# Two rows of the last chunk but one, stored by thirteen masked indirect transfers

## The chip, the cores and the metric

The kernel runs on one core of one Trainium2 chip. The metric is device time in microseconds of one execution; each comparison is between medians of several executions. The core has the engines that the profile calls DVE (VectorE), ACT (ScalarE), POOL (GpSimd), SP (SyncE, used here only to issue transfers) and PE (TensorE, unused here), and sixteen DMA engines that carry all transfers between the chip's main memory and the on-chip buffer of 128 partitions.

## What is computed

A softmax over rows of logits of shape (2, 8, 2112, 2112), after a bias that depends on the head and on the distance of row and column, clipped at 16:

```python
pos = np.arange(S)
rel_clipped = np.clip(pos[:, None] - pos[None, :], -16, 16) + 16
logits = logits + rel_bias[:, rel_clipped][None]
logits = logits - logits.max(axis=-1, keepdims=True)
exp = np.exp(logits)
return exp / exp.sum(axis=-1, keepdims=True)
```

All in float32. Every logit is read once and every result written once: 285 MB each way.

## The kernel before

The 33,792 rows are dealt out so that each partition owns 264 consecutive rows (`ROWS`). A chunk is six rows of each partition (`R`), 6,336 KB, and there are 44 chunks (`N`), numbered 0 to 43. Four buffers `X[0]` to `X[3]` (`NBUF`) hold chunks in turn; results are written in place, so a buffer is loaded, worked on, and stored from.

Work on a chunk: DVE adds the bias strip `F` and takes the negated row maximum (`add`, line 181), ACT exponentiates with the row sum as by-product (`exps`, line 190), DVE takes reciprocals and multiplies, three rows to a group (`scale`, lines 198 and 202). Each scaled row adds one to the semaphore `scaled`. Ahead of the loop DVE builds the bias table `M` from `rel_bias`, which ACT's queue loads at line 108; POOL contributes two index tables (lines 112 and 113).

All large transfers are issued by SP, in an order written out by hand. It loads chunk 0 row by row (line 99) and chunks 1 to 3 (line 103). Then it stores chunk 0: five rows of every partition in one transfer, and the sixth row by seventeen smaller ones, listed in `FAN`, of 15, 14, 13 ... 1 partitions, one row each (lines 223 to 232). Then a loop (line 233): store the next chunk when it is scaled, wait until the chunk stored before has landed (`st`), load the chunk that takes its buffer. After the loop stand the stores of chunks 41 and 42 (lines 238 and 239) and of chunk 43 in two halves of three rows (lines 240 and 241), so that the first half goes while the second is being scaled. `store` (line 91) waits on `scaled` and then issues. At the end SP waits for the stores still under way, last for the two halves on `landed` (line 244).

POOL, after its two index tables, waits for chunk 0's stores (lines 114 to 116) and passes that on to SP as `st[0]` (line 117). It has nothing after that.

Of the kernel before, what the change touches and what calls it, by code (L numbers as in the profile page):

```python
# [8 lines left out]
I32 = mybir.dt.int32  # L9
EXP = mybir.ActivationFunctionType.Exp  # L10
ALU = mybir.AluOpType
# [4 lines left out]
def kernel(  # L16
# [6 lines left out]
    nc = tc.nc  # L23
    P = 128
    B, H, S, S2 = logits.shape
# [3 lines left out]
    ROWS = B * H * S // P  # L29
    PB = S // ROWS  # L30
    assert ROWS * P == B * H * S and PB * ROWS == S and PB == H == 8
    R = 6
    NBUF = 4
    STEP = R * NBUF
    N = ROWS // R
# [2 lines left out]
    MW = S + ROWS - 1  # L38
    FW = S + STEP - 1
    BIG = 3.0e38  # L40
    LANES = 9
    FAN = []
    for lane in range(LANES):
        m = len(range(lane, P, LANES))
        k = 15 if lane == 0 else 15 - lane
# [4 lines left out]
    io = ctx.enter_context(tc.tile_pool(name="io", bufs=1))  # L50
    X = [io.tile([P, R * S], FP32, tag=f"X{b}", name=f"X{b}") for b in range(NBUF)]
# [2 lines left out]
    nmax = io.tile([P, STEP], FP32, tag="nmax", name="nmax")  # L54
    tot = io.tile([P, STEP], FP32, tag="tot", name="tot")
    rec = io.tile([P, STEP], FP32, tag="rec", name="rec")
    ip = io.tile([P, 3, PB], I32, tag="ip", name="ip")
    ps = ctx.enter_context(tc.tile_pool(name="ps", bufs=1, space=bass.MemoryType.PSUM))
    M = ps.tile([P, 4096], FP32, tag="M", name="M")

    def view(t, offset, dims):

        return bass.AP(tensor=t.tensor, offset=t.offset + offset, ap=[[list(t.ap[0])[0], P]] + dims)

    def rows(t, j, n):

        return bass.AP(tensor=t.tensor, offset=t.offset + j * S, ap=[[ROWS * S, P], [1, n * S]])

    with tc.tile_critical(no_gpsimd_drain=True):
        ld = [nc.alloc_semaphore(f"ld{b}") for b in range(NBUF)]  # L70
        st = [nc.alloc_semaphore(f"st{b}") for b in range(NBUF)]
        added = nc.alloc_semaphore("added")
        expd = nc.alloc_semaphore("expd")
        scaled = nc.alloc_semaphore("scaled")
# [2 lines left out]
        pre = nc.alloc_semaphore("pre")  # L77
        idx = nc.alloc_semaphore("idx")
        dve = nc.alloc_semaphore("dve")
        main = nc.alloc_semaphore("main")  # L80
        fan = [nc.alloc_semaphore(f"fan{i}") for i in range(2)]
        landed = tc.alloc_semaphore("landed")

        def take(eng, sem, n):
            eng.wait_ge(sem, n).then_inc(sem, -n)  # L85


        def load(j, b):
            nc.sync.dma_start(out=X[b][:, :], in_=rows(logits, j, R)).then_inc(ld[b], 16)

        def store(j, b, s0=0, n=R, sem=None):
            take(nc.sync, scaled, n)
            nc.sync.dma_start(
                out=rows(out, j + s0, n), in_=X[b][:, s0 * S : (s0 + n) * S]
            ).then_inc(sem or st[b], 16)


        for r in range(R):
            nc.sync.dma_start(
                out=X[0][:, r * S : (r + 1) * S], in_=rows(logits, r, 1)  # L100
            ).then_inc(ld[0] if r == R - 1 else pre, 16)
        for n in range(1, NBUF):
# [6 lines left out]
            out=rbB,  # L109
            in_=bass.AP(tensor=rel_bias.tensor, offset=rel_bias.offset, ap=[[0, P], [1, H * W]]),  # L110
        ).then_inc(rb, 16)
        nc.gpsimd.iota(ip[:, 0], pattern=[[0, PB]], base=0, channel_multiplier=1).then_inc(idx, 1)
        nc.gpsimd.iota(ip[:, 2], pattern=[[1, PB]], base=0, channel_multiplier=0).then_inc(idx, 1)  # L113
        take(nc.gpsimd, main, 16)
        take(nc.gpsimd, fan[0], 16 * ((len(FAN) + 1) // 2))
        take(nc.gpsimd, fan[1], 16 * (len(FAN) // 2))
        nc.gpsimd.sem_inc(st[0], 16)

        v = nc.vector
        done = [0]  # L120

        def then(ins):
            done[0] += 1
            ins.then_inc(dve, 1)

        def settle():
            v.wait_ge(dve, done[0])
# [6 lines left out]
                             op0=ALU.logical_shift_right, op1=ALU.bitwise_and))  # L134
# [6 lines left out]
        settle()  # L141
        for m, op in ((eq, ALU.is_equal), (gt, ALU.is_gt), (le, ALU.is_le), (lt, ALU.is_lt)):
            then(v.tensor_scalar(out=m, in0=dp, scalar1=0.0, scalar2=None, op0=op))  # L143
        v.wait_ge(rb, 16)
        settle()
        then(v.tensor_tensor(  # L146
            out=view(F, 0, [[W, H], [1, W]]), in0=view(F, 0, [[W, H], [1, W]]),
            in1=view(F, SC + 3 * PB, [[1, H], [0, W]]), op=ALU.mult))
        settle()
        then(v.tensor_reduce(out=rbS[:, :], in_=view(F, 0, [[1, W], [W, H]]),  # L150
                             axis=mybir.AxisListType.X, op=ALU.add))
# [5 lines left out]
            out=view(F, 0, [[W, PB], [1, W]]), in0=view(F, SC + 2 * PB, [[1, PB], [0, W]]),  # L157
            in1=view(rbS, W - 1, [[0, PB], [-1, W]]), op=ALU.mult))
# [6 lines left out]
            out=view(M, U, [[ROWS, PB], [1, W]]), in0=view(F, 0, [[W, PB], [1, W]]),  # L165
            in1=view(F, SC + 8 * PB, [[1, PB], [0, W]]), op=ALU.add))
        then(v.tensor_copy(out=view(M, U + W, [[ROWS, PB], [1, ROWS - W]]),  # L167
                           in_=view(F, SC + 7 * PB, [[1, PB], [0, ROWS - W]])))
# [8 lines left out]
        def add(b):  # L177
            take(v, ld[b], 16)
            for r in range(b * R, (b + 1) * R):
                x = X[b][:, (r - b * R) * S : (r - b * R + 1) * S]  # L180
                v.tensor_tensor_reduce(  # L181
                    out=x, in0=x, in1=F[:, STEP - 1 - r : STEP - 1 - r + S], scale=-1.0, scalar=BIG,
                    op0=ALU.add, op1=ALU.min, accum_out=nmax[:, r : r + 1],
# [37 lines left out]
        for i, (k, g, lane) in enumerate(FAN):  # L221
            p = g * LANES + lane
            nc.sync.dma_start(
                out=bass.AP(
                    tensor=out.tensor, offset=out.offset + (p * ROWS + R - 1) * S,
                    ap=[[LANES * ROWS * S, k], [1, S]],
                ),
                in_=bass.AP(
                    tensor=X[0].tensor, offset=X[0].offset + p * PSX + (R - 1) * S,
                    ap=[[LANES * PSX, k], [1, S]],  # L230
                ),
            ).then_inc(fan[i % 2], 16)
        with nc.Fori(0, ROWS - 2 * STEP + 1, STEP, engines=[ENG.SP]) as j:
            for b in range(NBUF):
                store(j + (b + 1) * R, (b + 1) % NBUF)
                take(nc.sync, st[b], 16)
                load(j + (b + NBUF) * R, b)
        for n in range(N - NBUF + 1, N - 1):
            store(n * R, n % NBUF)
        store((N - 1) * R, (N - 1) % NBUF, 0, HALF, landed)  # L240
        store((N - 1) * R, (N - 1) % NBUF, HALF, R - HALF, landed)
        for b in range(NBUF - 1):
            take(nc.sync, st[(N + b) % NBUF], 16)
    nc.sync.wait_ge(landed, nc.sync.to_reg(32), synchronizes=[nc.sync.lower_ap(out)])


# [28 lines left out]
```

## Time and profile before

| | us |
|---|---|
| median of 3 runs | 1331.55 |
| lowest and highest | 1331.31, 1331.82 |
| the profiled execution's own time | 1331.3 |
| its span, first to last instruction | 1329.5 |
| DVE busy | 976.7 |
| ACT busy | 575.2 |
| POOL busy | 0.4 |

The rows of the profile are shown in the prediction. How they read: the page begins with the span, then gives for each engine the busy time, its share and the number of instructions; a line of forty digits or numbers cuts the span into forty equal slices (a digit 9 is 90% busy or more; GB/s is what the DMA engines moved). A DMA queue's line has packets, MB and the share of sixteen engines' time; q1 is SP's queue and q10 ACT's. A packet is here one partition's part of a transfer, or the 4 bytes by which a DMA engine counts up a semaphore when its part is done. In a window's row stand the stretch (us from the span's start), its length, the busy time of DVE, ACT and POOL with their instructions, the clock of PE, the mean share of the sixteen DMA engines, and GB/s. In the timeline SPq and ACTq are the sequencers that issue transfers. A row of issues has the size of one transfer and the median time from issue to landing.

### The profile page before, as it was taken

How to read it: one execution, taken by the hardware profiler on the slowest of the kernel's cores; microseconds unless marked ns; L12 is line 12 of the kernel's file. 1: busy time of each engine (PE TensorE's matmuls, PEld its weight loads, DVE VectorE, ACT ScalarE, POOL GpSimd, SP SyncE). 2: the span in 40 equal slices, each digit the busy share in tenths (PEclk: the TensorE clock that was granted, in tenths of full speed). 3: DMA queues.
4: the chain of work that ended last, by engine and by line, in shares of the span. 5: the costliest groups of instructions: out<-in, count | busy, mean ns of one | idle time of the engine just before them, and what ended most of it. 6: DMA issues, size and time to landing. Idle time of an engine off the chain costs nothing. (4 is left out here: it accounts for less than half of the span.)

```text
span 1329.5 us, 2477 instructions
## 1 busy us (share of the span) xinstructions
DVE 976.7 (73%) x911; ACT 575.2 (43%) x539; POOL 0.4 (0%) x6
## 2 busy tenths in 40 slices
DVE  5998767777877776787778767677877776687772
ACT  2565333444444343345444333444444343345440
POOL 0000000000000000000000000000000000000000
DMA  9999999999999999999999999999999999999997
GB/s 391 427 426 424 436 430 433 438 433 435 432 435 435 433 436 430 436 433 435 430 433 439 433 433 427 439 435 432 433 432 438 430 433 430 436 430 436 438 432 337
DMA packets 13939, 571.12 MB, mean 430 GB/s; under 512 B 1648, under 2 KB 1776, under 8 KB 1776
## 3 DMA queue, kind: packets, MB, share of 16 engines
q1 hardware_dynamic: 13792, 570.96, 99.5%
q10 hardware_dynamic: 144, 0.14, 0.1%
q14 instruction: 3, 0.02, 0.0%
HBM read 285.61 MB, written 285.47 MB: 430 GB/s over the span
## 5 line engine op out<-in xcount | busy, mean ns | idle before, releaser
L181 DVE CUSTOM_DVE_ANT_0 X<-X,F 128x2112 f32<-128x2112 f32 x264 | 605.2, 2354 | 302.0 <-DVEq L85 302.0
L190 ACT ACTIVATE X<-X,nmax 128x2112 f32<-128x2112 f32 x264 | 541.7, 2052 | 538.2 <-ACTq L85 516.4
L202 DVE TENSOR_SCALAR X<-X,rec 128x2112 f32<-128x2112 f32 x264 | 332.5, 1316 | 13.2
L190 ACT ACT_TABLE_LOAD x11 | 14.1, 1283 | 185.8 <-ACTq L85 185.8
L190 ACT ACTIVATION_READ_ACCUMULATOR X<-X,nmax 128x1 f32 x264 | 49.2, 186 | 0.0
L175 DVE COPY F<-M 128x2135 f32 x11 | 26.1, 2375 | 6.6 <-DVEq L85 6.6
L181 DVE DVE_READ_ACCUMULATOR2_ANT nmax<- 128x1 f32 x264 | 21.7, 82 | 0.0
L198 DVE RECIPROCAL rec<-tot 128x3 f32<-128x3 f32 x88 | 15.0, 170 | 0.0
L146 DVE TENSOR_TENSOR F<-F 128x264 f32<-128x264 f32 x1 | 0.4, 435 | 4.9 <-DMA F<-in_rel_bias_dram 4.9
L167 DVE COPY M<-F 128x1848 f32<-128x1848 f32 x1 | 2.1, 2077 | 0.0
L133 DVE TENSOR_SCALAR ip<-ip 128x8 int32<-128x8 int32 x1 | 0.2, 172 | 1.3 <-POOL ip L113 1.3
L150 DVE TENSOR_REDUCE rbS<-F 128x33 f32<-128x264 f32 x1 | 0.6, 610 | 0.0
L164 DVE TENSOR_TENSOR M<-F 128x264 f32<-128x264 f32 x1 | 0.4, 441 | 0.0
L156 DVE TENSOR_TENSOR F<-F,rbS 128x264 f32<-128x264 f32 x1 | 0.4, 426 | 0.0
L143 DVE TENSOR_SCALAR F<-F 128x8 f32<-128x8 f32 x4 | 0.4, 167 | 0.0
L169 DVE COPY M<-rbS 128x247 f32<-128x247 f32 x1 | 0.4, 406 | 0.0
L154 DVE TENSOR_SCALAR F<-F,rbS 128x8 f32<-128x8 f32 x1 | 0.2, 231 | 0.0
L160 DVE SCALAR_TENSOR_TENSOR F<-F,rbS 128x8 f32<-128x8 f32 x1 | 0.2, 227 | 0.0
L155 DVE TENSOR_SCALAR F<-F,rbS 128x8 f32<-128x8 f32 x1 | 0.2, 225 | 0.0
L161 DVE SCALAR_TENSOR_TENSOR F<-F,rbS 128x8 f32<-128x8 f32 x1 | 0.2, 221 | 0.0
L136 DVE TENSOR_TENSOR F<-ip 128x8 f32<-128x8 int32 x1 | 0.2, 167 | 0.0
L139 DVE TENSOR_TENSOR F<-ip 128x8 f32<-128x8 int32 x1 | 0.2, 167 | 0.0
(9 smaller groups left out, 1.2 us busy)
## 6 DMA issues: line engine op xcount, KB each, us to landing
X<-in_logits_dram SPq DMA_DIRECT2D x43, 6336.0 KB, 44.7
out_dram<-X SPq DMA_DIRECT2D x42, 6336.0 KB, 52.8
X<-in_logits_dram SPq DMA_DIRECT2D x6, 1056.0 KB, 12.6
out_dram<-X SPq DMA_DIRECT2D x2, 3168.0 KB, 21.9
out_dram<-X SPq DMA_DIRECT2D x1, 5280.0 KB, 34.9
F<-in_rel_bias_dram ACTq DMA_DIRECT2D x1, 132.0 KB, 6.4
out_dram<-X SPq DMA_DIRECT2D x1, 123.8 KB
out_dram<-X SPq DMA_DIRECT2D x1, 115.5 KB
```

What stands on the lines that cost most here:

```text
L143: then(v.tensor_scalar(out=m, in0=dp, scalar1=0.0, scalar2=None, op0=op))
L146: then(v.tensor_tensor(out=view(F, 0, [[W, H], [1, W]]), in0=view(F, 0, [[W, H], [1, W]]), in1=view(F, SC + 3 * PB, [[1, H], [0, W]]), op= ...
L150: then(v.tensor_reduce(out=rbS[:, :], in_=view(F, 0, [[1, W], [W, H]]), axis=mybir.AxisListType.X, op=ALU.add))
L156: then(v.tensor_tensor(out=view(F, 0, [[W, PB], [1, W]]), in0=view(F, SC + 2 * PB, [[1, PB], [0, W]]), in1=view(rbS, W - 1, [[0, PB], [-1, ...
L164: then(v.tensor_tensor(out=view(M, U, [[ROWS, PB], [1, W]]), in0=view(F, 0, [[W, PB], [1, W]]), in1=view(F, SC + 8 * PB, [[1, PB], [0, W]] ...
L167: then(v.tensor_copy(out=view(M, U + W, [[ROWS, PB], [1, ROWS - W]]), in_=view(F, SC + 7 * PB, [[1, PB], [0, ROWS - W]])))
L169: then(v.tensor_copy(out=M[:, 0:U], in_=low.to_broadcast([P, U])))
L175: v.tensor_copy(out=F[:, :], in_=M[:, bass.ds(ROWS - STEP - j, FW)]).then_inc(dve, 1)
L181: v.tensor_tensor_reduce(out=x, in0=x, in1=F[:, STEP - 1 - r : STEP - 1 - r + S], scale=-1.0, scalar=BIG, op0=ALU.add, op1=ALU.min, accum_ ...
L190: nc.scalar.activation(out=x, in_=x, func=EXP, scale=-1.0, bias=nmax[:, r : r + 1], accum_out=tot[:, r : r + 1],).then_inc(expd, 1)
L198: v.reciprocal(out=rec[:, r0 : r0 + HALF], in_=tot[:, r0 : r0 + HALF]).then_inc(inv, 1)
L202: v.tensor_scalar_mul(out=x, in0=x, scalar1=rec[:, r : r + 1]).then_inc(scaled, 1)
```

## The change

Of chunk 42, the last but one, SP stores only the first four rows of each partition. The last two rows (`PAIR`) go by POOL's queue in thirteen indirect transfers. Each takes 16 consecutive partitions, from `p0` on, and writes for each of them one piece of two rows (16.5 KB) to the row pair of the output that an index table names. Element e of a transfer is partition p0 + e. A mask of 16 bits for each transfer says which of its elements are wanted; the index of the others is raised by `FAR`, over the bound, and an index over the bound is passed over without an error. The thirteen ranges overlap, and each of the 128 partitions is wanted exactly once, so the list `PLAN` settles at which place e of a transfer each partition's piece goes.

The tables are made at the start: POOL writes masks and indices by 13 memsets and 14 iotas, DVE waits for them and then shifts, masks, multiplies and subtracts in four small instructions, ahead of its wait for the bias. POOL waits on a new semaphore, `ready`, which SP raises when chunk 42 is scaled, and issues the thirteen transfers. SP waits at the end for their 13 x 16 counts on `soft` too.

```diff
+    PLAN = [(0, 49095), (3, 26631), (12, 65472), (23, 55264), (34, 65509), (45, 32736), (54, 65472),
+            (65, 64480), (75, 15873), (81, 65287), (92, 57312), (103, 31716), (112, 65474)]
+    PAIR = 2
+    FAR = 1 << 20
+    assert sorted(p0 + e for p0, m in PLAN for e in range(16) if m >> e & 1) == list(range(P))
...
+        g = nc.gpsimd
+        BLK = ROWS // PAIR
+        AT = ((N - 1) * R - PAIR) // PAIR
+        made = [0]
+
+        def step(ins):
+            made[0] += 1
+            ins.then_inc(pool, 1)
+
+        for w, (p0, m) in enumerate(PLAN):
+            step(g.memset(bit[:, w : w + 1], m))
+            step(g.iota(sel[:, w : w + 1], pattern=[[0, 1]], base=p0 * BLK + AT + FAR, channel_multiplier=BLK))
+        step(g.iota(lan[:, :], pattern=[[0, len(PLAN)]], base=0, channel_multiplier=1))
         take(nc.gpsimd, main, 16)
         take(nc.gpsimd, fan[0], 16 * ((len(FAN) + 1) // 2))
         take(nc.gpsimd, fan[1], 16 * (len(FAN) // 2))
         nc.gpsimd.sem_inc(st[0], 16)
+        take(g, ready, 1)
+        pairs = out.rearrange("b h s t -> (b h s t)").rearrange("(n c) -> n c", c=PAIR * S)
+        late = X[(N - 2) % NBUF]
+        lap = list(late.ap[0])[0]
+        for w, (p0, m) in enumerate(PLAN):
+            g.indirect_dma_start(
+                out=pairs, out_offset=bass.IndirectOffsetOnAxis(ap=sel[:, w : w + 1], axis=0),
+                in_=bass.AP(tensor=late.tensor, offset=late.offset + p0 * lap + (R - PAIR) * S,
+                            ap=[[lap, 16], [1, PAIR * S]]),
+                in_offset=None, bounds_check=B * H * S // PAIR - 1, oob_is_err=False,
+            ).then_inc(soft, 16)
...
+        take(v, pool, made[0])
+        then(v.tensor_tensor(out=bit[:, :], in0=bit[:, :], in1=lan[:, :], op=ALU.logical_shift_right))
+        settle()
+        then(v.tensor_scalar(out=bit[:, :], in0=bit[:, :], scalar1=1, scalar2=None, op0=ALU.bitwise_and))
+        settle()
+        then(v.tensor_scalar(out=bit[:, :], in0=bit[:, :], scalar1=FAR, scalar2=None, op0=ALU.mult))
+        settle()
+        then(v.tensor_tensor(out=sel[:, :], in0=sel[:, :], in1=bit[:, :], op=ALU.subtract))
         v.wait_ge(rb, 16)
...
-        for n in range(N - NBUF + 1, N - 1):
+        for n in range(N - NBUF + 1, N - 2):
             store(n * R, n % NBUF)
+        take(nc.sync, scaled, R)
+        nc.sync.sem_inc(ready, 1)
+        nc.sync.dma_start(
+            out=rows(out, (N - 2) * R, R - PAIR), in_=X[(N - 2) % NBUF][:, 0 : (R - PAIR) * S]
+        ).then_inc(st[(N - 2) % NBUF], 16)
         store((N - 1) * R, (N - 1) % NBUF, 0, HALF, landed)
         store((N - 1) * R, (N - 1) % NBUF, HALF, R - HALF, landed)
         for b in range(NBUF - 1):
             take(nc.sync, st[(N + b) % NBUF], 16)
+    nc.sync.wait_ge(soft, nc.sync.to_reg(16 * len(PLAN)), synchronizes=[nc.sync.lower_ap(out)])
     nc.sync.wait_ge(landed, nc.sync.to_reg(32), synchronizes=[nc.sync.lower_ap(out)])
```

More of the change, by code (lines that the diff above doesn't have):

```diff
@@ L56 @@
     rec = io.tile([P, STEP], FP32, tag="rec", name="rec")
+    sel = io.tile([16, len(PLAN)], I32, tag="sel", name="sel")
+    bit = io.tile([16, len(PLAN)], I32, tag="bit", name="bit")
+    lan = io.tile([16, len(PLAN)], I32, tag="lan", name="lan")
     ip = io.tile([P, 3, PB], I32, tag="ip", name="ip")
@@ L79 @@
         dve = nc.alloc_semaphore("dve")
+        ready = nc.alloc_semaphore("ready")
+        pool = nc.alloc_semaphore("pool")
+        soft = tc.alloc_semaphore("soft")
         main = nc.alloc_semaphore("main")
```

## The prediction

> **What bounds the kernel now.** I read the page first, then SP's waits, then the end of the timeline, and last the final ten microseconds in slices. The page (span, busy times, DMA by fortieths of the span, queues), then SP's longest waits:
>
> ```profile
> span 1329.5 us, 2477 instructions
> DVE 976.7 (73%) x911; ACT 575.2 (43%) x539; POOL 0.4 (0%) x6
> DMA  9999999999999999999999999999999999999997
> GB/s 391 427 426 424 436 430 433 438 433 435 432 435 435 433 436 430 436 433 435 430 433 439 433 433 427 439 435 432 433 432 438 430 433 430 436 430 436 438 432 337
> q1 hardware_dynamic: 13792, 570.96, 99.5%
> ...
> SPq L244 <- DMA out_dram<-X: 14.6, 1, 14.6
> ```
>
> No compute engine is full; the sixteen DMA engines are, 99.5% of the span on SP's queue alone, at some 430 GB/s. Only the last fortieth is lower (337 GB/s), and the program ends by a wait of SP for the last store. So the time is the bytes at that rate plus what is lost at the two ends; bytes do not change here, so the change can act only at the ends. The end on the timeline:
>
> ```profile
> 1238.15 0.35 SPq L89 DMA_DIRECT2D X<-in_logits_dram  x1
> 1244.93 60.38 SPq L93 DMA_DIRECT2D out_dram<-X  x4
> ...
> 1271.08 3.78 DVE L202 TENSOR_SCALAR X<-X,rec 128x2112 f32<-128x2112 f32 x3
> 1283.08 2.36 DVE L181 CUSTOM_DVE_ANT_0 X<-X,F 128x2112 f32<-128x2112 f32 x1 [8.22 <-DVEq L85]
> ...
> 1297.08 3.78 DVE L202 TENSOR_SCALAR X<-X,rec 128x2112 f32<-128x2112 f32 x3
> ...
> 1301.09 3.78 DVE L202 TENSOR_SCALAR X<-X,rec 128x2112 f32<-128x2112 f32 x3
> ```
>
> The last load, issued at 1238.15, has landed at 1283.08; the last chunk but one is scaled at 1271.08 + 3.78 = 1274.9 and the last chunk at 1304.9, when SP issues its last half. From there only transfers run. Their end in slices (the last two columns are the DMA engines' mean share and GB/s), then the packets that start after 1320, then those of one late microsecond:
>
> ```profile
> 1316.00:1318.00 2.00, 0.00 (x0) 0.00 (x0) 0.00 (x0) 1.00 0.97 418
> 1318.00:1320.00 2.00, 0.00 (x0) 0.00 (x0) 0.00 (x0) 1.00 1.09 469
> 1320.00:1321.00 1.00, 0.00 (x0) 0.00 (x0) 0.00 (x0) 1.00 0.77 329
> 1321.00:1322.00 1.00, 0.00 (x0) 0.00 (x0) 0.00 (x0) 1.00 0.59 253
> 1322.00:1323.00 1.00, 0.00 (x0) 0.00 (x0) 0.00 (x0) 1.00 0.41 177
> 1323.00:1324.00 1.00, 0.00 (x0) 0.00 (x0) 0.00 (x0) 1.00 0.41 177
> 1324.00:1325.00 1.00, 0.00 (x0) 0.00 (x0) 0.00 (x0) 1.00 0.24 101
> 1325.00:1326.00 1.00, 0.00 (x0) 0.00 (x0) 0.00 (x0) 1.00 0.18 76
> 1326.00:1327.00 1.00, 0.00 (x0) 0.00 (x0) 0.00 (x0) 1.00 0.06 25
> 1327.00:1328.00 1.00, 0.00 (x0) 0.00 (x0) 0.00 (x0) 1.00 0.06 25
> 1328.00:1329.50 1.50, 0.00 (x0) 0.00 (x0) 0.00 (x0) 1.00 0.00 0
> ...
> DMA packets 63, 1.17 MB, mean 123 GB/s; under 512 B 17, under 2 KB 17, under 8 KB 17
> q1 hardware_dynamic: 63, 1.17, 28.5%
> ...
> DMA packets 1, 0.03 MB, mean 25 GB/s; under 512 B 0, under 2 KB 0, under 8 KB 0
> q1 hardware_dynamic: 1, 0.03, 5.9%
> ```
>
> This is the point on which all else hangs. A share is booked to the slice in which a packet starts, which is why one reads 1.09. Up to 1320 all sixteen engines work; then they run out one after another, and from 1326 on a single one works (0.06 is one sixteenth). One packet of a half store, 24.75 KB (three rows), takes 5.9% of 16 engines in 1 us: 0.94 us. The last starts after 1327, so the last engine ends at about 1328.1, and 1.4 us follow to the span's end. The same work spread evenly: packets starting after 1320 are 28.5% of 16 engines over 9.5 us, so 0.285 x 9.5 = 2.71 us for each engine, plus on average half a packet (0.47) under way at 1320: 1323.2. **4.9 us of the end is imbalance between DMA engines.**
>
> **The change part by part.** *Removed from SP's queue:* two of six rows of the last store but one, on every engine alike. *Added:* the same rows on POOL's queue, 128 pieces of two rows (16.5 KB), handed out by the table's masks. Counted by bit, engines 0 to 15 get 5, 4, 5, 0, 0, 6, 10, 10, 11, 12, 10, 12, 12, 11, 11, 9 pieces, where each had 8. A piece is two thirds of the packet above: 0.63 us. An engine that gets none ends 8 x 0.63 = 5.0 us sooner: the latest, 1328.1, comes to 1323.1. An engine that gets twelve ends 4 x 0.63 = 2.5 us later: those that run dry first, about 1320.9, come to 1323.4. So the table's extremes agree with the windows' extremes, and its sum is that of an even end near 1323.2.
>
> Does it hit the right engines? No view names an engine. The packet records behind the views can be followed, since on one engine each starts as its predecessor ends, and engines told apart by how many of the one-row pieces of the FAN stores each moved. The latest ends then lie on the engines that get fewest pieces, the earliest on those that get most; the exception is an engine that ends late and still gets ten. This moves my chances only.
>
> *Misfit.* That engine ends where the share drops from 0.41 to 0.24, at about 1324.1; two pieces more make it 1325.4. Lags of other executions will differ a little too, and now many engines stand near the maximum instead of one. Bounds: 0 (even end) to 2.0 (that engine alone sets the end, against 1323.4). I take 0.9, since not each execution need have such an engine.
>
> *Packets.* Each piece and each of thirteen completions costs something fixed. The only second queue with small packets is ACT's, in the first 20 us:
>
> ```profile
> q10 hardware_dynamic: 144, 0.14, 4.5%
> ```
>
> 4.5% of 16 engines over 20 us is 14.4 us for 144 packets, 0.10 each, 0.04 of it bytes at the rate above. So at most 0.06 x 25 = 1.5 us on an engine with twelve pieces, at least nothing; I take 0.3, being nearer to the low end because these packets are sixteen times as large and their neighbours sit in a full queue.
>
> *Issue by POOL.* No row shows a transfer issued by POOL. Nearest rows: SP's issue, and the store and half stores from issue to landing:
>
> ```profile
> L93 SPq DMA_DIRECT2D out_dram<-X x5: 332/337/338, 1215.0 to 1305.0; - x5
> ...
> out_dram<-X SPq DMA_DIRECT2D x1, 6336.0 KB, 38.6
> out_dram<-X SPq DMA_DIRECT2D x2, 3168.0 KB, 21.9
> F<-in_rel_bias_dram ACTq DMA_DIRECT2D x1, 132.0 KB, 6.4
> ```
>
> Low: 0.34 us each, 4.4 us in all. High: POOL handles one only after the other has landed, 6.4 us as for ACT's small load, 83 us. POOL is released at 1274.9 and the last piece must be through by 1323.2; with one SP packet ahead (0.94) and its own 0.63 that leaves 1321.6 - 1274.9 = 46.7 us, 3.6 us each. Below that the issue costs nothing, hidden by SP's backlog; from 4.0 us each ((1328.1 - 1.6 - 1274.9) / 13) the change loses. I take 1.5 us each, nearer to SP's row, since nothing in the code makes POOL wait for a landing: the last is issued at 1294.4. Without the cover of the backlog it would cost 19.5 us plus.
>
> [...]
>
> *Moved past the last load.* The pieces enter from 1274.9, while the last load (landed 1283.08) is on the engines, and may delay it by at most their whole work, 5.0 us a mean engine; then the first half store goes at about 1305.9 instead of 1300.9. The store issued at 1274.95 lands 38.6 us later, at 1313.5; with a third of its 15 us gone, 1308.5. The queue stays covered by 2.6 us. Cost: nothing; without that cover up to 5.0.
>
> *Added waits.* POOL's wait for "ready" holds only the thirteen transfers. SP's wait is that of the removed store. The wait at the end for "soft" stands beside the one for the last halves.
>
> *Start.* 27 small POOL instructions and four DVE instructions ahead of the bias:
>
> ```profile
> 1.04 0.13 POOL L112 IOTA ip<- 128x8 int32 x1 [0.59 <-PEq L270]
> 1.13 0.14 POOL L113 IOTA ip<- 128x8 int32 x1
> ...
> 2.07 0.39 DVE L143 TENSOR_SCALAR F<-F 128x8 f32<-128x8 f32 x4
> 7.39 0.43 DVE L146 TENSOR_TENSOR F<-F 128x264 f32<-128x264 f32 x1 [4.93 <-DMA F<-in_rel_bias_dram]
> ...
> 19.04 2.38 DVE L175 COPY F<-M 128x2135 f32 x1 [6.58 <-DVEq L85]
> ```
>
> 27 x 0.14 = 3.8 us after 1.3 gives 5.1; four dependent steps of about 0.2 give 5.9, before the bias lands at 7.39. Were it later, DVE still has 6.58 us idle ahead of 19.04. Cost: nothing, up to 8 us of delay.
>
> *Sum.* Last transfer: 1323.4 + 0.9 + 0.3 = 1324.6 against 1328.1: 3.5 us less. The profiled execution took 1331.3 us (span 1329.5 and 1.8 around it), so 1327.8; the median of the runs is 1331.55, 0.25 above it, so **1328.1**.
>
> **Rivals.** *The table does not steer (slower).* If the slots that the masks refuse are dropped before the transfer is shared out, the first engines get a piece of nearly every transfer; if they are moved all the same, every engine gets thirteen. Either way the latest engine has 13 pieces for 8: 5 x 0.63 = 3.15 us more, **1334.7**. It decides as soon as the latest engine gets more than eight. For it: no refused slot is in the trace. Against: the masks fit the slices' ends, which a compacted share would make pointless.
>
> *POOL is too slow (slower).* At 5 us an issue the last one comes at 1274.9 + 65 = 1339.9 and ends 1.6 us later, 13.4 us after 1328.1: **1345**. For it: nothing of POOL's DMA is seen. Against: it needs more than 4.0 us, twelve times SP's 0.34.
>
> *POOL is shut out while DVE works.* Add and scale fill DVE from 1283.08 to 1304.87. If POOL issues nothing in that time, four go before (8.2 us at 2 us, a high choice) and nine after, to 1322.9, ending at 1324.5: still hidden, a gain of 3.5. [...]
>
> *The lags are not the same each time (no change).* If they reshuffle, some engine with ten to twelve pieces is 3 to 4 us late and ends near 1327.5: **1330.9**. For it: the one exception. Against: three runs within 0.5 us, as if one engine set the end each time.
>
> **How the numbers follow.** Forecast 0.62, table not steering 0.13, POOL too slow 0.12, lags reshuffled 0.13; the shut-out belongs to the forecast. About 0.2% (2.7 us, below 1328.9) can be told from no change. Nine tenths of the forecast and a little of the rest are faster: 0.57; slower are the two slow rivals with a little of the reshuffle: 0.26; 0.17 remains. The forecast's own range is 1326.6 (the even end, a gain of 4.9) to 1330.3 (misfit 2.0 and packets 1.5: an end at 1326.9). The whole range reaches up to the table that doesn't steer: 1326.6 to 1334.8.
>
> **What would show it.** Right: the slices after 1320 hold full share to about 1322.5 and fall to zero by 1324.6; 1.17 MB after 1320 grows, the end comes sooner; POOL's issues lie between 1275 and 1305; POOL's queue carries 2.2 MB in 128 pieces. Wrong: 208 pieces or 3.5 MB there; POOL's last issue after 1321; a load landing after 1288 with a dip of DMA share near 1308; one engine alone after 1326 again.

## The result and the profile after

The changed kernel takes 1339.41 us (median; 1337.33 to 1339.56) against 1331.55: a ratio of 1.0055, interval 1.0040 to 1.0069. It is slower by 7.9 us, where 3.5 us less were forecast. The profiled execution has a span of 1337.8 us, 8.3 more than before. Its page, the span, POOL's busy time and the queues (q0 is POOL's):

```profile
span 1337.8 us, 2541 instructions
DVE 977.4 (73%) x915; ACT 575.2 (43%) x539; POOL 20.8 (2%) x46
GB/s 389 428 430 420 436 432 433 435 432 436 433 435 432 435 430 433 435 433 436 433 429 432 432 436 435 435 433 433 426 433 433 435 436 436 436 433 432 427 383 288
q1 hardware_dynamic: 13792, 568.79, 98.7%
q0 software_dynamic: 416, 2.16, 0.7%
```

Little has changed up to the last three fortieths; there 427, 383 and 288 GB/s stand for 438, 432 and 337. POOL's queue moved just the 2.16 MB that it should, so refused slots carried no data. POOL's issues beside DVE's work, in order of time:

```profile
1276.31 0.96 POOL L147 DMA_INDIRECT out_dram<-X,sel  x1 [1273.54 <-POOLq L96]
1277.57 0.85 POOL L147 DMA_INDIRECT out_dram<-X,sel  x1 [0.30 <-issue]
...
1283.42 2.36 DVE L224 CUSTOM_DVE_ANT_0 X<-X,F 128x2112 f32<-128x2112 f32 x1 [8.24 <-DVEq L96]
1284.47 2.03 POOL L147 DMA_INDIRECT out_dram<-X,sel  x1 [0.30 <-issue]
...
1295.92 2.92 POOL L147 DMA_INDIRECT out_dram<-X,sel  x1 [0.30 <-issue]
```

POOL was done at 1298.8, and the last load landed at 1283.4, 0.3 us later than before. Neither is the cause. The last stage in slices, with the DMA engines' mean share and GB/s last in each row:

```profile
1295.00:1300.00 5.00, 4.85 (x6) 4.30 (x4) 3.54 (x2) 1.00 1.00 311
1300.00:1305.00 5.00, 4.85 (x5) 0.00 (x0) 0.00 (x0) 1.00 0.93 345
1305.00:1310.00 5.00, 0.22 (x1) 0.00 (x0) 0.00 (x0) 1.00 0.99 373
1310.00:1315.00 5.00, 0.00 (x0) 0.00 (x0) 0.00 (x0) 1.00 0.99 341
1315.00:1320.00 5.00, 0.00 (x0) 0.00 (x0) 0.00 (x0) 1.00 0.98 368
...
1326.00:1327.00 1.00, 0.00 (x0) 0.00 (x0) 0.00 (x0) 1.00 0.81 296
1329.00:1330.00 1.00, 0.00 (x0) 0.00 (x0) 0.00 (x0) 1.00 0.47 203
1335.00:1336.00 1.00, 0.00 (x0) 0.00 (x0) 0.00 (x0) 1.00 0.12 51
```

This is the finding: the engines are as busy as before (share 0.93 to 1.00), but they move 311 to 373 GB/s where 418 (at a share of 0.97) and 469 (at 1.09) stand in the rows of before from 1316 to 1320. The packets themselves take longer. And the end is no more even: from 1326 it runs out over some ten microseconds.

The loss can be measured by one number, engine time for each MB: the queues' shares in the window from 1270 to 1340, times 16 engines and 70 us, over the MB moved. Before, then after:

```profile
q1 hardware_dynamic: 654, 22.61, 74.7%
```

```profile
q1 hardware_dynamic: 655, 20.50, 71.4%
q0 software_dynamic: 416, 2.16, 13.5%
```

Before: 0.747 x 1120 / 22.61 = 37.0 us for each MB. After: 0.849 x 1120 / 22.66 = 42.0. The excess is 4.96 x 22.66 = 112 us of engine time, **7.0 us for each of sixteen engines**, nearly the whole rise. Somewhat over a third of it falls on SP's packets (39.0 us for each MB), the rest on the pieces (70.0), which took 0.135 x 1120 / 128 = 1.18 us each and not 0.63.

### The profile page after: what moved, and what is told of

The parts are those of the page before. It is cut to its first block, busy times and chain, and to the rows that moved or that the text cites. A ratio compares the mean times of both kernels' runs of the same rounds, so it can differ in the third digit from the quotient of the medians.

```text
span 1337.8 us, 2541 instructions
## 1 busy us (share of the span) xinstructions
DVE 977.4 (73%) x915; ACT 575.2 (43%) x539; POOL 20.8 (2%) x46
## 3 DMA queue, kind: packets, MB, share of 16 engines
q0 software_dynamic: 416, 2.16, 0.7%
HBM read 285.61 MB, written 286.83 MB: 428 GB/s over the span
## 5 line engine op out<-in xcount | busy, mean ns | idle before, releaser
L233 ACT ACT_TABLE_LOAD x11 | 14.1, 1283 | 185.9 <-ACTq L96 185.9
L147 POOL DMA_INDIRECT out_dram<-X,sel x13 | 18.9, 1453 | 1277.2 <-POOLq L96 1273.5
```

Source lines behind the costliest of these rows:

```text
L147: g.indirect_dma_start(out=pairs, out_offset=bass.IndirectOffsetOnAxis(ap=sel[:, w : w + 1], axis=0), in_=bass.AP(tensor=late.tensor, offs ...
L233: nc.scalar.activation(out=x, in_=x, func=EXP, scale=-1.0, bias=nmax[:, r : r + 1], accum_out=tot[:, r : r + 1],).then_inc(expd, 1)
```

## Experiments

**Which difference slows the packets?** Theory P: a piece is read by a DMA engine that does not read this partition in SP's transfers, beside the engine that does. Theory Q: the second queue. Rival C: the cutting into small transfers with refused slots. Three runs separate them. The first moves the same pieces without POOL (SP's store of the first four rows and the wait at the end are as in the changed kernel):

```diff
+        for w in range(8):
+            nc.sync.dma_start(
+                out=bass.AP(tensor=out.tensor, offset=out.offset + (16 * w * ROWS + (N - 1) * R - PAIR) * S,
+                            ap=[[ROWS * S, 16], [1, PAIR * S]]),
+                in_=bass.AP(tensor=late.tensor, offset=late.offset + 16 * w * lap + (R - PAIR) * S,
+                            ap=[[lap, 16], [1, PAIR * S]]),
+            ).then_inc(soft, 16)
```

> The same 128 two-row pieces of chunk 42, but issued by SP as eight transfers of 16 consecutive partitions, no POOL transfer, no masks, eight pieces for each DMA engine. Theory P (a piece is slow because its DMA engine reads a partition that another engine reads at the same time as part of its own share): packets stretch as in the changed kernel, some 5 us or more of lost time for each engine on average between 1275 us and the end, time 1335 to 1341 us. Theory Q (a second, software-fed queue beside SP's slows the engines): no second queue here, so no stretched packets and 1331 to 1332 us.

Measured: 1337.84 us against 1331.38, ratio 1.0047 (1.0030 to 1.0064). Window 1270 to 1340 of it, and two slices:

```profile
q1 hardware_dynamic: 909, 22.56, 84.6%
```

```profile
1300.00:1305.00 5.00, 4.56 (x5) 0.00 (x0) 0.00 (x0) 1.00 1.07 257
1305.00:1310.00 5.00, 0.00 (x0) 0.00 (x0) 0.00 (x0) 1.00 0.96 220
```

42.0 us for each MB, as in the changed kernel, with one queue and no refused slot; while the eight transfers run, full engines move 220 GB/s. So neither the second queue nor the refused slots are needed for the loss; the cutting is still there. The second run has POOL's queue and SP's partitions (again with the four-row store and the wait):

```diff
+        take(nc.gpsimd, ready, 1)
+        nc.gpsimd.dma_start(
+            out=rows(out, (N - 1) * R - PAIR, PAIR), in_=X[(N - 2) % NBUF][:, (R - PAIR) * S : R * S]
+        ).then_inc(soft, 16)
```

> The same two rows, issued by POOL as one plain transfer of 128 partitions, so that every DMA engine should get the same partitions as in SP's 128-partition transfers. Theory P: no stretch, 1331 to 1332.5 us. Theory Q: packets stretch on both queues, 1335 to 1340 us.

Measured: 1331.43 us, ratio 1.0001 (0.9991 to 1.0010). Its window 1270 to 1340:

```profile
q1 hardware_dynamic: 652, 20.34, 67.3%
q0 software_dynamic: 144, 2.16, 7.2%
```

0.745 x 1120 / 22.50 = 37.1 us for each MB: no loss. The third keeps masks and indirect transfers, and changes who reads what:

```diff
-    PLAN = [(0, 49095), (3, 26631), (12, 65472), (23, 55264), (34, 65509), (45, 32736), (54, 65472),
-            (65, 64480), (75, 15873), (81, 65287), (92, 57312), (103, 31716), (112, 65474)]
+    PLAN = [(b + c, m) for c in range(4) for b, m in ((0, 255), (32, 65535), (64, 65280))]
...
-                            ap=[[lap, 16], [1, PAIR * S]]),
+                            ap=[[4 * lap, 16], [1, PAIR * S]]),
```

(The index's step is multiplied by 4 likewise.)

> The changed kernel with another table: twelve masked indirect transfers by POOL, 64 of 192 slots refused, each piece given to the DMA engine that reads that partition in SP's transfers too, if a 128-partition transfer gives engine e of the first eight the partitions 4e to 4e+3 and 32+4e to 32+4e+3, and the others likewise from 64 on. Eight pieces for each engine. Theory P: no stretch, 1331 to 1333 us, the end as uneven as before. Theory Q, and rival C (the cutting into many small transfers with refused slots): as in the changed kernel, some 6 us lost, 1336 to 1340 us.

Measured: 1331.78 us, ratio 1.0004 (0.9994 to 1.0013). Its window:

```profile
q1 hardware_dynamic: 653, 20.39, 67.5%
q0 software_dynamic: 384, 2.16, 7.4%
```

37.2 us for each MB. Twelve masked transfers by POOL cost next to nothing (0.3 us an engine); theory P is left. Which partitions an engine moves in a 128-partition transfer is an assumption, the one that stands behind the "if" of the expectation above; no view names an engine. What the runs show for it is the loss: 0.3 us an engine with this table, which follows it, and in the runs below 1.2 us where 31 pieces depart from it, 2.1 where 50 do, 5.2 to 7.0 where 117 to 120 do. I call an engine's partitions by this assumption its own, or its share, and a piece foreign that another engine reads, slot e of a transfer being counted to engine e: 117 of 128 in the changed kernel, 120 in the first run.

**Is it the reading or the writing?** A foreign piece is also written where another engine's rows lie in main memory. This run is the third with the pieces written to the places of partition 127 - p, so the last two rows of chunk 42 do not stand where the softmax has them:

```diff
-            step(g.iota(sel[:, w : w + 1], pattern=[[0, 1]], base=p0 * BLK + AT + FAR, channel_multiplier=4 * BLK))
+            step(g.iota(sel[:, w : w + 1], pattern=[[0, 1]], base=(P - 1 - p0) * BLK + AT + FAR, channel_multiplier=-4 * BLK))
```

> The run in which every DMA engine reads its own partitions (1331.78 us), but each piece is written to the place in the output that belongs to partition 127 - p, so that the last two rows of chunk 42 stand in other places than in the reference. The engine then reads its own partitions and writes where another engine's partitions are stored. If the cost of foreign pieces arises where the partitions are read: no stretch, 1331 to 1332.5 us. If it arises where the output is written (one engine's region of main memory): 5 to 7 us of stretch an engine, 1336 to 1340 us.

Measured: 1331.88 us against 1331.47, ratio 1.0004 (0.9994 to 1.0013). Its window:

```profile
q1 hardware_dynamic: 657, 20.60, 68.2%
q0 software_dynamic: 384, 2.16, 7.4%
```

37.2 us for each MB, as in the third run. Writing to another engine's region costs nothing here, so the cost arises where the partitions are read. The converse (foreign read, own region) was not tried.

**Foreign reading, or crowding?** By the count above, the changed kernel reads up to four partitions of one engine's share in one transfer, by four engines. This run, shown against the first, takes another step and has two instead of four, and 120 foreign pieces again:

```diff
-                in_=bass.AP(tensor=late.tensor, offset=late.offset + 16 * w * lap + (R - PAIR) * S,
-                            ap=[[lap, 16], [1, PAIR * S]]),
+                in_=bass.AP(tensor=late.tensor, offset=late.offset + (16 * w - 15 * (w % 2)) * lap + (R - PAIR) * S,
+                            ap=[[2 * lap, 16], [1, PAIR * S]]),
```

> As the run with eight SP transfers of 16 consecutive partitions (6.9 us stretch an engine, 1337.84 us), but with every second partition of 32, so that 2 and not 4 slots of a transfer lie in the share of one engine. As many foreign pieces as there: 120 of 128. If foreign reading alone costs: the same, 6 to 7 us an engine and 1337 to 1339 us. If the crowding of slots on one share costs: a third to a half of it, 1333 to 1335 us.

Measured: 1339.48 us, ratio 1.0060 (1.0045 to 1.0076), and in its window:

```profile
q1 hardware_dynamic: 915, 22.86, 82.9%
```

40.6 us for each MB, 5.2 us an engine against 7.0. Neither expectation is met: halving the crowding takes off a quarter of the loss. That does not make the rest a cost of foreign reading as such, since two slots still meet on each share; the FAN stores, below, read foreign partitions with one slot to a share, and lose little. The time is not shorter than in the first run, though less is lost: the latest engine sets it and not the mean. Between 1334.75 and 1336.5 us this run still starts one packet of 25 KB (14 GB/s), and the first run none; why an engine is later here stays open.

**Can the end be evened at all?** Two more tables give every engine just as many pieces as the changed kernel does, but with few foreign ones. Their entries carry a step: 16 partitions four apart, or one apart.

```diff
...
+    PLAN = [(0, 4, 54247), (1, 4, 20455), (2, 4, 16103), (3, 4, 15335), (5, 1, 32640),
+            (20, 4, 63840), (25, 4, 65216), (34, 4, 65473), (35, 4, 65476), (64, 4, 65504),
+            (65, 4, 65472), (66, 4, 65280), (67, 4, 65280)]
```

> The changed kernel with another table, issued at the same moment: again thirteen transfers and the same number of pieces for each DMA engine (5, 4, 5, 0, 0, 6, 10, 10, 11, 12, 10, 12, 12, 11, 11, 9), but in twelve of them the 16 slots are four partitions apart, so that a transfer reads from all over the partitions, and 78 of 128 pieces go to the engine that reads that partition in SP's transfers too. Theory P1 (a group of partitions gives one engine's rate, whoever reads; what a foreign engine reads is taken from the owner): the 50 foreign pieces cost each about 1.26 us of engine time beyond their own, 2 to 4 us an engine, and the late groups of partitions stay late: 1331 to 1335 us. Theory P2 (only the crowding of one transfer's slots on 16 neighbouring partitions costs): below 1 us an engine, and the steering works: 1327.5 to 1329.5 us.

Measured: 1330.78 us against 1331.54, ratio 0.9995 (0.9985 to 1.0004). Its window 1270 to 1340:

```profile
q1 hardware_dynamic: 654, 20.44, 68.8%
q0 software_dynamic: 416, 2.16, 8.9%
```

38.5 us for each MB, 2.1 us an engine for 50 foreign pieces. P2 falls, with its loss below 1 us and its 1327.5 to 1329.5 us. Of P1 the loss is met at the low end of its 2 to 4 us, but with about 0.7 us a foreign piece and not 1.26, and the time cannot be told from that of before. Sixteen transfers allow 97 own pieces:

```diff
...
+    PLAN = [(0, 4, 13287), (1, 1, 26624), (1, 4, 6375), (2, 4, 8167), (3, 4, 16359),
+            (4, 1, 49664), (9, 4, 16836), (16, 4, 193), (32, 4, 65472), (33, 4, 65248),
+            (34, 4, 65504), (35, 4, 65472), (64, 4, 65280), (65, 4, 65280), (66, 4, 65280),
+            (67, 4, 65280)]
```

> The spread table with sixteen transfers instead of thirteen, same moment as the changed kernel and same counts for each DMA engine, now 97 of 128 pieces to the engine that owns the partition (78 before). If each foreign piece costs what the 50 did (1.9 us an engine in all, 0.6 us each): 31 x 0.6 / 16 = 1.2 us an engine and 1330.0 us; if only the crowded slots cost, below that, 1329 to 1330 us. If the number of transfers costs: 1331 us or more.

Measured: 1330.37 us against 1331.50, ratio 0.9991 (0.9982 to 1.0000). Its window:

```profile
q1 hardware_dynamic: 652, 20.34, 68.2%
q0 software_dynamic: 512, 2.16, 7.8%
```

37.8 us for each MB, 1.2 us an engine for 31 foreign pieces, as expected, and the three added transfers cost nothing that can be seen. The pieces took 0.078 x 1120 / 128 = 0.68 us each, counting packets included, and 0.65 in the third run, where all are own. So most foreign pieces are hardly longer here; the larger part of the loss is on SP's packets beside them (37.6 us for each MB against 37.1 in the third run).

**Beside loads.** Three runs move the pieces to chunk 41 and release POOL when the store of chunk 40 has landed, so that they begin while the owners still write their partitions:

```diff
-        AT = ((N - 1) * R - PAIR) // PAIR
+        AT = ((N - 2) * R - PAIR) // PAIR
...
-        late = X[(N - 2) % NBUF]
+        late = X[(N - 3) % NBUF]
...
+        take(nc.sync, scaled, R)
+        nc.sync.dma_start(
+            out=rows(out, (N - 3) * R, R - PAIR), in_=X[(N - 3) % NBUF][:, 0 : (R - PAIR) * S]
+        ).then_inc(st[(N - 3) % NBUF], 16)
+        take(nc.sync, st[N % NBUF], 16)
+        nc.sync.sem_inc(ready, 1)
+        store((N - 2) * R, (N - 2) % NBUF)
```

> The table of the run before (spread slots, steering counts), but for the last two rows of chunk 41, and POOL is released when chunk 40 has landed (about 1268 us), so that most pieces run beside the last load, in which the owners write to their partitions instead of reading them. Theory P1 with reads and writes apart: less than 1 us of stretch an engine, and the steering works: 1327.5 to 1329.5 us. P1 with reads and writes sharing one rate: 2 to 4 us of stretch, 1331 to 1335 us. P2: as in the run before, 1327.5 to 1329.5 us.

> The changed kernel's own table (16 neighbouring partitions a transfer), moved like the run before to chunk 41 and beside the last load. If the crowding within a transfer costs by itself: pieces stretch to 1.2 us and more, 2 us or more an engine, 1330 to 1334 us. If only the collision with the owners' reads costs: 1327.5 to 1329.5 us.

> The sixteen-transfer table for chunk 41, beside the last load. With 1.27 us an engine for 50 foreign pieces in that place: 0.8 us for 31, and 1329.5 to 1330.2 us; the best so far if the steering holds.

The windows 1270 to 1340, in this order:

```profile
q1 hardware_dynamic: 655, 20.50, 68.6%
q0 software_dynamic: 416, 2.16, 8.4%
```

```profile
q1 hardware_dynamic: 654, 20.44, 70.5%
q0 software_dynamic: 416, 2.16, 12.1%
```

```profile
q1 hardware_dynamic: 655, 20.50, 68.3%
q0 software_dynamic: 512, 2.16, 7.8%
```

Worked out alike, these are 38.1, 40.9 and 37.6 us for each MB. But they test less than was meant. In the first two of them DVE begins to add at 1283.1, as soon as the last load has landed, and up to 1283 only a quarter of the pieces has been started. Window 1270 to 1283 of these two:

```profile
q1 hardware_dynamic: 125, 4.75, 84.5%
q0 software_dynamic: 92, 0.57, 10.7%
```

```profile
q1 hardware_dynamic: 127, 4.80, 86.2%
q0 software_dynamic: 92, 0.51, 14.3%
```

That is 34 and 30 pieces. With the spread table they took 0.107 x 16 x 13 / 34 = 0.65 us each, as own pieces do, and SP's packets 37.0 us for each MB: beside the load nothing is lost, as theory P1 with reads and writes apart expects. With the changed kernel's table they took 0.99, and SP's packets 37.4; whether they crowd each other there or meet the first reads of the next store stays open. The rest of what these runs lose, they lose after the load has landed, so their times decide nothing about reads beside writes. All runs that move pieces:

| pieces of two rows | foreign | lost, us an engine | for each foreign piece, us | time, us (before beside it) | ratio, interval |
|---|---|---|---|---|---|
| changed kernel | 117 | 7.0 | 0.96 | 1339.41 (1331.55) | 1.0055 (1.0040 to 1.0069) |
| SP, 16 consecutive | 120 | 7.0 | 0.94 | 1337.84 (1331.38) | 1.0047 (1.0030 to 1.0064) |
| SP, every second | 120 | 5.2 | 0.69 | 1339.48 (1331.50) | 1.0060 (1.0045 to 1.0076) |
| POOL, one plain transfer | 0 | 0.1 | – | 1331.43 (1331.38) | 1.0001 (0.9991 to 1.0010) |
| POOL, own | 0 | 0.3 | – | 1331.78 (1331.38) | 1.0004 (0.9994 to 1.0013) |
| POOL, own, written elsewhere | 0 | 0.3 | – | 1331.88 (1331.47) | 1.0004 (0.9994 to 1.0013) |
| spread table | 50 | 2.1 | 0.68 | 1330.78 (1331.54) | 0.9995 (0.9985 to 1.0004) |
| 97 own | 31 | 1.2 | 0.60 | 1330.37 (1331.50) | 0.9991 (0.9982 to 1.0000) |
| changed table, chunk 41 | 117 | 5.6 | 0.76 | 1339.28 (1331.54) | 1.0065 (1.0048 to 1.0081) |
| spread table, chunk 41 | 50 | 1.5 | 0.48 | 1330.62 (1331.54) | 0.9992 (0.9982 to 1.0001) |
| 97 own, chunk 41 | 31 | 0.9 | 0.45 | 1329.27 (1331.50) | 0.9984 (0.9975 to 0.9993) |

(Lost: the excess over 37.0 us for each MB, times the MB, over 16. For each foreign piece: that times 16, over their number.)

On the average of a run a foreign piece of chunk 42 costs 0.60 to 0.69 us, about its own length once more (0.63), and half as much again (0.94 and 0.96) where up to four crowd on one share. In the runs with POOL's masked transfers 0.3 us of the loss is there without any foreign piece, so the spread tables' pieces cost rather less. What fits all rows, by this count, is that engines slow each other where they read one share at the same time. No run has foreign pieces at this moment with only one engine on each share; the FAN stores have to stand in for it.

The last row is faster than both kernels. Its end in slices:

```profile
1321.00:1322.00 1.00, 0.00 (x0) 0.00 (x0) 0.00 (x0) 1.00 0.94 406
1322.00:1323.00 1.00, 0.00 (x0) 0.00 (x0) 0.00 (x0) 1.00 0.82 355
1323.00:1324.00 1.00, 0.00 (x0) 0.00 (x0) 0.00 (x0) 1.00 0.47 203
1324.00:1325.00 1.00, 0.00 (x0) 0.00 (x0) 0.00 (x0) 1.00 0.12 51
```

Before, the share fell from 0.77 to nothing over eight microseconds; here from 0.94 over four. This is the even end that the prediction counted on, and it takes the same counts for each engine as in the changed kernel. So the counts were about right, and what spoilt them was who reads which partition. How much of the 2.2 us comes from the earlier moment was not separated; with this table at the changed kernel's own moment, 1.1 us are won, at the edge of the interval.

**Where does the unevenness come from?** One run takes the FAN stores away:

```diff
-        take(nc.sync, scaled, R)
-        nc.sync.dma_start(out=rows(out, 0, R - 1), in_=X[0][:, 0 : (R - 1) * S]).then_inc(main, 16)
...
+        store(0, 0)
```

> The kernel before with chunk 0 stored whole by one transfer instead of five rows and seventeen FAN pieces. The FAN pieces put up to 9 one-row packets (0.32 us each) more on the first engines and 8 fewer on the last. Without them the latest engine (given 13 of 128, 5 above its share) should end about 1.3 to 1.6 us sooner: 1329.5 to 1330.5 us. Theory P expects the stretched packets of 75 to 98 us to go too (about 0.6 us an engine); theory Q says nothing of them, since one queue alone is at work there.

Measured: 1330.55 us against 1331.38, ratio 0.9993 (0.9984 to 1.0003), just above the range expected, and no change that can be told. Its window from 75 to 98 us, and the same of the kernel before:

```profile
q1 hardware_dynamic: 225, 9.78, 98.3%
```

```profile
q1 hardware_dynamic: 464, 9.87, 102.0%
```

Over 16 x 23 us these are 37.0 against 38.0 us for each MB: with the FAN stores 0.6 us an engine is lost, in a kernel with no second queue. But most of it is not lost on the pieces. Windows 75 to 83 and 90 to 98 of the kernel before:

```profile
q1 hardware_dynamic: 324, 3.58, 106.3%
```

```profile
q1 hardware_dynamic: 80, 3.24, 99.2%
```

The pieces run in the first of these windows: 38.0 us for each MB, 0.2 us an engine, counting packets included. In the second none is left (from 83 to 90 all 60 packets are already of six rows, 3.04 MB), and there it is 39.2, or 0.4 us an engine; what costs that stays open. By the count used above, 115 of the 128 FAN pieces are foreign, but no two of one transfer lie in the same engine's share. So foreign reading that is spread over the shares costs little, and theory P needs the meeting on one share that it names. The end, without the FAN stores, stays uneven:

```profile
1320.00:1321.00 1.00, 0.00 (x0) 0.00 (x0) 0.00 (x0) 1.00 0.48 203
1327.00:1328.00 1.00, 0.00 (x0) 0.00 (x0) 0.00 (x0) 1.00 0.06 25
```

In the microsecond from 1320 half the engines start nothing (0.48), and one still works at 1327 (0.06). The FAN stores are not the main cause of the lags; which is, stays open.

## Why the prediction was wrong

The step that failed is in the count of pieces: "A piece is two thirds of the packet above: 0.63 us." It took the time of a piece from its bytes alone. In the changed kernel it was 1.18 us, and SP's packets beside it grew too, 7.0 us an engine in all. The prediction has no term for two engines that read one share at the same time, and its misfit of 0.9 and packet cost of 0.3 do not cover it. The packet cost itself was well sized: 0.3 us an engine in the run with own partitions.

The rest, step by step. *What bounds the kernel* held. The 4.9 us of unevenness are borne out in part: with 97 own pieces in chunk 41, 2.2 us are won. *The table hits the right engines* held, by the even end of the same run. *Issue by POOL*: 0.84 to 2.92 us for 1.5 taken, hidden. *Moved past the last load*: 0.3 us, no cost. *Start*: the four table steps were over before the bias landed:

```profile
3.50 0.16 DVE L186 TENSOR_TENSOR sel<-sel,bit 16x13 int32<-16x13 int32 x1
7.32 0.43 DVE L189 TENSOR_TENSOR F<-F 128x264 f32<-128x264 f32 x1 [3.65 <-DMA F<-in_rel_bias_dram]
```

Of the rivals, the table that does not steer would have left 13 pieces on an engine; the 2.16 MB exclude the form in which refused slots are moved, and the even end with the same counts the form in which they are dropped first. POOL was not too slow. The side of "slower" was right for two rivals, but by neither mechanism: the one that fits the runs was missing. The sign was in the change itself, which reads 16 neighbouring partitions with 16 engines. The rows of before gave no price for it: the FAN stores, which read foreign partitions too, lose only 0.2 us an engine while they run.

## What to carry to other kernels

When work is moved between DMA engines, ask not only how much each gets but which partitions it then reads, and who reads there at the same time: here a piece that another engine read cost 0.60 to 0.96 us of engine time in chunk 42, about its own length (0.63) once more or half as much again, part of it on SP's packets beside it (39.0 us for each MB in the changed kernel, 37.0 before). Move only the difference and leave all else with its owner (28 foreign pieces would be the least for these counts; the changed kernel has 117, the fastest run 31). And read share and GB/s together: a share of 0.96 at 220 GB/s, where 0.97 had stood for 418, was here what showed engines in each other's way.

## What the runs showed of the hardware that was not expected

A refused slot of an indirect transfer was not free of packets: POOL's queue has 416 packets for 128 pieces in thirteen transfers, 384 in twelve, 512 in sixteen. After the pieces there remain 288, 256 and 384, which is as many as one for each slot (208, 192, 256) and one for each refused slot (80, 64, 128) make. In the changed kernel's trace all 288 are of 4 bytes, the size of a counting packet, and in all three runs the queue's MB are the pieces' alone (2.16). The profile page's line of memory traffic goes another way: it has 286.83 MB written where before has 285.47, and the difference, 1.35 ahead of rounding, is 80 pieces of 16.5 KB; with 128 refused slots (97 own, chunk 41) it has 287.64. So that line seems to count the refused slots as written, which the queue's packets do not.

POOL's issue takes 0.84 to 0.96 us before DVE's adds begin and 1.97 to 2.03 us while DVE adds the bias (line 224); the one that runs from the last add into the scaling takes 2.92. The prediction's rival had adding and scaling shut POOL out altogether: the issues beside both were longer, but they went on, the last of thirteen done at 1298.8 with DVE at work from 1283.4.
